# A LoRA linear layer on one core: the last row of each partition of the first chunk stored by fifteen small stores, and lora_B loaded in one transfer

## The chip, the core and the metric

The kernel runs on one core of a Trainium2 chip. The metric is the device time in microseconds (us), the median of several runs: 164.36 us before the change (three runs, 164.32 to 164.52).

The core has five engines with queues of their own: PE (TensorE, matrix products), DVE (VectorE), ACT (ScalarE), POOL (GpSimd) and SP (SyncE, which here only issues transfers). Transfers between DRAM and the core's memory (SBUF) are done by sixteen DMA engines. An engine that issues a transfer goes on at once; the transfer adds to a semaphore when it has landed, 16 in all.

## What is computed

```
x_flat = x.reshape(-1, 256)              # 32768 rows
y = x_flat @ W                           # W: 256 x 256
lora_out = ((x_flat @ lora_A) * lora_E) @ lora_B      # rank 16
y = y + scale * lora_out                 # float32, scale = 1
```

x and the output are 33.55 MB each. The weights are small: W is 256 KB, lora_A and lora_B 16 KB each, lora_E 64 bytes.

## The kernel before

**One weight.** A prologue folds the low-rank path into W: lora_A is transposed on PE (L125), scaled by lora_E on DVE (`ate`, L129), multiplied by lora_B on PE (L134) and added to W (`weff`, L138). Then each row of x takes one product with `weff`.

**Chunks and slots.** The rows are cut into nine chunks (`PLAN`, L5): the first and last have 16 rows for each of the 128 partitions (2 MB), the seven between have 32 (4 MB). In chunk i, partition p holds `b = PLAN[i]` consecutive rows of 256 floats, so what one partition loads or stores is one run of 16 or 32 KB in DRAM and in SBUF (`rows_of`, L46). There are six slots of 32 rows (L56). A chunk is loaded into its slot, and its result overwrites it there (L201) and is stored from it.

**Inside a chunk** the work goes by groups of 4 rows: DVE rounds 8 rows to bf16 (L148), PE transposes 4 (L162), DVE copies the transposed rows from PSUM (L154), PE multiplies (L173), ACT copies the result from PSUM to the slot (L201).

**The order of the transfers** is written out by hand. All big ones are issued by SP, into one queue (q1 in the profile), which spreads each over the sixteen DMA engines, 8 packets of 16 or 32 KB and a 4-byte packet for the semaphore on each; each engine takes its packets in order.

- SP first issues W (L101) and loads 0 to 5 (`load`, L88), all six slots, in the first 4.5 us.
- Then, as chunks are finished, it waits for ACT's last copy of chunk i and issues store i (`store`, L91).
- After store 2 it issues loads 6, 7 and 8 (`AFTER`, L8). Each takes the slot of chunk 0, 1 or 2, so SP waits first until that store has landed (L212).
- Then come stores 3 to 8, and at the end SP waits for all stores (L94, L224).

ACT issues the small loads on a second queue (q10): lora_A (L102), lora_B in four transfers over rows 0 to 1, 2 to 4, 5 to 8 and 9 to 15 (`B_PARTS`, L12 and L103), and lora_E (L105). DVE waits for lora_B before L121 and for lora_E before L129.

`Count` (L18) keeps a semaphore and the total that was added to it so far; `by` adds to it when an instruction or transfer is done.

Of the kernel before, what the change touches and what calls it, by code (L numbers as in the profile page):

```python
# [4 lines left out]
PLAN = [16] + [32] * 7 + [16]  # L5
ROWS, SLOTS = 32, 6
# [2 lines left out]

G, ROUND = 4, 4  # L10

B_PARTS = [(0, 2), (2, 5), (5, 9), (9, 16)]  # L12
P = 128
FP32 = mybir.dt.float32
BF16 = mybir.dt.bfloat16
# [15 lines left out]
def kernel(tc, x, W, lora_A, lora_B, lora_E, scale, out):  # L31
    nc = tc.nc
    x_flat = x.flatten_outer_dims()
    out_flat = out.flatten_outer_dims()
# [11 lines left out]
    def rows_of(flat, i):  # L46
        b, r0 = PLAN[i], starts[i]
        return flat[r0:r0 + b * P, :].rearrange("(p b) k -> p b k", b=b)
# [28 lines left out]
    s_st = [Count(nc, f"s_st{i}") for i in range(len(PLAN))]  # L77
# [6 lines left out]
    def slot(i):  # L84
        return slots[i % SLOTS][:, :PLAN[i], :]

    def load(i):
        s_ld[i].by(nc.sync.dma_start(out=slot(i), in_=rows_of(x_flat, i)), 16)  # L88

    def store(i):  # L90
        s_st[i].by(nc.sync.dma_start(out=rows_of(out_flat, i), in_=slot(i)), 16)  # L91

    def spent(engine, count):
        engine.wait_ge(count.sem, count.total).then_inc(count.sem, -count.total)  # L94
# [5 lines left out]
    with tc.tile_critical(no_gpsimd_drain=True):  # L100
        s_w.by(nc.sync.dma_start(out=w_sb, in_=W.rearrange("(c p) m -> p c m", p=P)), 16)  # L101
        s_a.by(nc.scalar.dma_start(out=a_sb, in_=lora_A.rearrange("(c p) r -> p c r", p=P)), 16)  # L102
        for lo, hi in B_PARTS:  # L103
            s_b.by(nc.scalar.dma_start(out=b_sb[lo:hi, :], in_=lora_B[lo:hi, :]), 16)
# [9 lines left out]
        out=ident, in_=ident, compare_op=mybir.AluOpType.not_equal, fill=1.0, base=0,  # L114
# [9 lines left out]
    for c in range(KC):  # L124
# [5 lines left out]
        out=ate, in0=ps_at, scalar1=e_sb, scalar2=float(scale),  # L130
# [68 lines left out]
    for g, (i, r) in enumerate(groups):  # L199
        nc.scalar.wait_ge(s_m.sem, g + 1)  # L200
        y = nc.scalar.copy(out=slot(i)[:, r:r + G, :], in_=ps_y[g % 2])  # L201
        if r + G < PLAN[i]:
            y.then_inc(can_y, 1)
        else:
            done = s_y.by(y)
            if g + 1 < NG:
                nc.scalar.wait_ge(s_y.sem, done)
                nc.scalar.sem_inc(can_y, 1)
            nc.sync.wait_ge(s_y.sem, done)
            store(i)  # L210
            for later in AFTER.get(i, []):
                nc.sync.wait_ge(s_st[later - SLOTS].sem, 16)  # L212
                load(later)


# [44 lines left out]
```

## Time and profile before

| | us |
|---|---|
| median of three runs | 164.36 (164.32 to 164.52) |
| the profiled execution | 164.26 |
| its span, first to last instruction | 162.86 |
| PE, DVE, ACT busy | 92.9, 79.3, 66.1 |
| store 0 issued; landed on the first and the last DMA engine | 24.82; 62.52 and 64.97 |
| load 6 issued | 64.99 |
| store 8 issued; landed on the first and the last DMA engine | 129.44; 159.37 and 162.82 |

The profile is that of one execution. Its page gives the busy time of each engine, and the span in 40 slices of 4.07 us, where a digit is the busy share in tenths. "DMA" is the mean share of the sixteen DMA engines. A row of the waits reads "who waited <- for what: us in total, times, longest". A row of the timeline has the start, the duration, the engine, the line, the operation, and in brackets the idle time before it and what ended it. A row of the windows has a stretch, its length, the busy time of the five rows PE, PEld (PE's weight loads), DVE, ACT and POOL with their instructions, the clock granted to PE, the DMA engines' share (counted by the packets that start in the stretch, so it can pass 1) and GB/s. The trace keeps a record of each DMA packet too: queue, start, duration and bytes.

### The profile page before, as it was taken

The numbers are of one execution on the slowest core, as the hardware profiler recorded it, in microseconds if no ns is written. First come the engines' busy times: TensorE is split into PE (matmuls) and PEld (weight loads), VectorE is DVE, ScalarE is ACT, GpSimd is POOL, SyncE is SP. The second block draws the span as 40 slices with busy tenths as digits, with TensorE's granted clock in tenths as the row PEclk, the third lists the DMA queues.
The fourth block names the chain that finished last, engine by engine and source line by source line (L and its number), as shares of the span: only waits on it lengthen the run. The fifth ranks groups of instructions, "written<-read, shape, count | busy, mean of one in ns | idle before, by whom it ended". The sixth has DMA issues, their size and how long they took to land. (4 is left out here: it accounts for less than half of the span.)

```text
span 162.9 us, 2602 instructions
## 1 busy us (share of the span) xinstructions
PE 92.9 (57%) x1028; PEld 82.0 (50%) x1028; DVE 79.3 (49%) x99; ACT 66.1 (41%) x65; POOL 1.0 (1%) x7
## 2 busy tenths in 40 slices
PE   0104989999999999998000039999999400000000
PEld 0003778898898889887000028889889300000000
DVE  0017589888888988892000082988895100000000
ACT  0300267777777777777000004677777600000000
POOL 0100000000000000000000000000000000000000
PEclk9999999999999999999955555999999975555555
DMA  5999999999999989999999999999999999999992
GB/s 145 421 439 475 402 427 467 394 475 419 394 485 402 386 382 463 427 419 445 427 419 459 419 435 402 443 459 427 427 443 427 423 445 427 427 443 419 406 439 89
DMA packets 3204, 67.45 MB, mean 414 GB/s; under 512 B 624, under 2 KB 896, under 8 KB 896
## 3 DMA queue, kind: packets, MB, share of 16 engines
q1 hardware_dynamic: 2864, 67.37, 97.0%
q10 hardware_dynamic: 336, 0.03, 0.2%
q8 instruction: 1, 0.02, 0.0%
q14 instruction: 3, 0.02, 0.0%
HBM read 33.85 MB, written 33.55 MB: 414 GB/s over the span
## 5 line engine op out<-in xcount | busy, mean ns | idle before, releaser
L201 ACT COPY xy<-psum_y 128x1024 f32<-128x1024 f32 x64 | 64.8, 1012 | 57.7 <-PE psum_y L173 57.7
L173 PE MATMUL psum_y<-weff,xt 128*128 128x256 bf16 x512 | 68.8, 279 | 21.7 <-PEq L97 20.1
L173 PEld LDWEIGHTS psum_y<-weff,xt 128*128 128x128 bf16 x512 | 47.6, 100 | 29.7 <-issue 24.3
L154 DVE COPY xt<-psum_xt 128x1024 bf16<-128x1024 bf16 x64 | 43.8, 687 | 14.6 <-PE psum_xt L162 14.5
L148 DVE CAST xb<-xy 128x2048 bf16<-128x2048 f32 x32 | 38.9, 1218 | 20.8 <-DMA xy<-in_x_dram 20.8
L162 PE MATMUL psum_xt<-ident_bf,xb 128*128 128x128 bf16 x512 | 40.8, 226 | 2.1 <-PEq L97 2.1
L162 PEld LDWEIGHTS psum_xt<-ident_bf,xb 128*128 128x128 bf16 x512 | 35.7, 102 | 4.2 <-issue 2.5
L121 DVE CAST b_bf<-xb 16x256 bf16<-16x256 f32 x1 | 0.3, 280 | 9.5 <-DMA xb<-in_lora_B_dram 9.5
L125 PE MATMUL ps_at<-ident,a_sb 128*16 128x128 f32 x2 | 0.6, 394 | 6.8 <-POOL ident_bf L117 6.8
L201 ACT ACT_TABLE_LOAD x1 | 1.3, 1283 | 5.6 <-PEq L109 5.6
L125 PEld LDWEIGHTS ps_at<-ident,a_sb 128*16 128x16 f32 x2 | 0.1, 88 | 6.7 <-issue 6.7
L134 PE MATMUL ps_aeb<-b_bf,ate 16*128 16x256 bf16 x2 | 0.6, 400 | 5.0 <-DVE ate L129 5.0
L134 PEld LDWEIGHTS ps_aeb<-b_bf,ate 16*128 16x128 bf16 x2 | 0.1, 106 | 5.5 <-DVE ate L129 5.5
L129 DVE TENSOR_SCALAR ate<-ps_at,e_sb 16x256 bf16<-16x256 f32 x1 | 0.5, 472 | 2.0 <-DMA e_sb<-in_lora_E_dram 2.0
L138 DVE TENSOR_TENSOR weff<-xb,ps_aeb 128x512 bf16<-128x512 f32 x1 | 0.7, 686 | 0.8 <-PE ps_aeb L134 0.8
L113 POOL TENSOR_SCALAR_AFFINE_SELECT ident<-ident 128x128 f32<-128x128 f32 x1 | 0.3, 292 | 0.2 <-POOL ident L111 0.2
L117 POOL CAST ident_bf<-ident 128x128 bf16<-128x128 f32 x1 | 0.3, 289 | 0.1
L111 POOL MEMSET ident<- 128x128 f32 x1 | 0.2, 204 | 5.1 <-POOLq L109 5.1
L241 POOL MEMSET const-bfloat16-1.0<- 128x1 bf16 x1 | 0.1, 101 | 0.0
L241 POOL MEMSET const-uint8-127<- 128x1 uint8 x1 | 0.1, 101 | 0.0
L241 POOL MEMSET const-float32-0.0<- 128x1 f32 x1 | 0.1, 98 | 0.2 <-issue 0.2
L241 POOL MEMSET const-float32-1.0<- 128x1 f32 x1 | 0.1, 99 | 0.0
## 6 DMA issues: line engine op xcount, KB each, us to landing
xy<-in_x_dram SPq DMA_DIRECT2D x7, 4096.0 KB, 29.1
out_dram<-xy SPq DMA_DIRECT2D x7, 4096.0 KB, 36.9
xy<-in_x_dram SPq DMA_DIRECT2D x2, 2048.0 KB, 16.3
out_dram<-xy SPq DMA_DIRECT2D x2, 2048.0 KB, 36.8
xb<-in_W_dram SPq DMA_DIRECT2D x1, 256.0 KB, 2.9
a_sb<-in_lora_A_dram ACTq DMA_DIRECT2D x1, 16.0 KB, 3.1
xb<-in_lora_B_dram ACTq DMA_DIRECT2D x1, 2.0 KB
xb<-in_lora_B_dram ACTq DMA_DIRECT2D x1, 3.0 KB
```

The lines of the kernel that those rows point to most:

```text
L113: s_id.by(nc.gpsimd.affine_select(out=ident, in_=ident, compare_op=mybir.AluOpType.not_equal, fill=1.0, base=0, pattern=[[-1, P]], channel ...
L117: s_id.by(nc.gpsimd.tensor_copy(out=ident_bf, in_=ident))
L125: at_done = nc.tensor.transpose(ps_at[:, c, :], a_sb[:, c, :], ident)
L129: s_v.by(nc.vector.tensor_scalar(out=ate, in0=ps_at, scalar1=e_sb, scalar2=float(scale), op0=mybir.AluOpType.mult, op1=mybir.AluOpType.mult))
L134: aeb_done = nc.tensor.matmul(ps_aeb[:, c, :], ate[:, c, :], b_bf, start=True, stop=True)
L138: s_v.by(nc.vector.tensor_add(out=weff, in0=w_sb, in1=ps_aeb))
L148: nc.vector.tensor_copy(out=xb[t % 2], in_=slot(i)[:, r:r + 2 * G, :]).then_inc(can_t, 1)
L154: nc.vector.tensor_copy(out=xt[g % 2], in_=ps_xt[g % 2]).then_inc(can_m, 1)
L162: done = nc.tensor.transpose(ps_xt[k % 2][:, j, c, :], xb[k // 2 % 2][:, k % 2 * G + j, c * P:(c + 1) * P], ident_bf)
L173: done = nc.tensor.matmul(ps_y[k % 2][:, j, :], xt[k % 2][:, j, c, :], weff[:, c, :], start=(c == 0), stop=(c == KC - 1))
L201: y = nc.scalar.copy(out=slot(i)[:, r:r + G, :], in_=ps_y[g % 2])
L241: nc = _bacc.Bacc("TRN2", target_bir_lowering=False, num_devices=1)
```

## The change

Chunk 0's store becomes sixteen stores: one of the first 15 rows of each of the 128 partitions, and then, for the last row of each partition, fifteen over 15, 14, 13, 12, 11, 10, 9, 9, 8, 7, 6, 5, 4, 3 and 2 partitions, 128 in all. They have one semaphore, so the wait before load 6 is for the total of 256 and no longer for 16. For loads 7 and 8 the total is 16 as before. lora_B is loaded by one transfer over its 16 rows in the place of four. Nothing else differs.

```diff
-B_PARTS = [(0, 2), (2, 5), (5, 9), (9, 16)]
+B_PARTS = [(0, 16)]
+
+SMALL = [15, 14, 13, 12, 11, 10, 9, 9, 8, 7, 6, 5, 4, 3, 2]
...
     def store(i):
-        s_st[i].by(nc.sync.dma_start(out=rows_of(out_flat, i), in_=slot(i)), 16)
+        to, y, b = rows_of(out_flat, i), slot(i), PLAN[i]
+        if i:
+            s_st[i].by(nc.sync.dma_start(out=to, in_=y), 16)
+            return
+        s_st[i].by(nc.sync.dma_start(out=to[:, :b - 1, :], in_=y[:, :b - 1, :]), 16)
+        p = 0
+        for n in SMALL:
+            s_st[i].by(nc.sync.dma_start(out=to[p:p + n, b - 1, :], in_=y[p:p + n, b - 1, :]), 16)
+            p += n
+        assert p == P
...
-                nc.sync.wait_ge(s_st[later - SLOTS].sem, 16)
+                nc.sync.wait_ge(s_st[later - SLOTS].sem, s_st[later - SLOTS].total)
```

## The prediction

> **What bounds the kernel now.** I read the page's slices and queue table first, then the waits of SP, then a table of windows over the tail, and last the single DMA packets.
>
> ```profile
> DMA  5999999999999989999999999999999999999992
> ...
> q1 hardware_dynamic: 2864, 67.37, 97.0%
> ```
>
> The sixteen DMA engines are busy in every slice from the second to the last but one, and SP's queue q1 alone fills 97.0% of their time. PE is at 57% and DVE at 49%. So the kernel is a queue of 67.4 MB; compute matters only if it lets that queue run dry. It doesn't, by SP's own waits:
>
> ```profile
> SPq L91 <- ACT xy L201: 83.5, 7, 19.3
> SPq L88 <- DMA out_dram<-xy: 36.3, 3, 17.6
> ```
>
> SP issues store 0 at 24.82 us, but the packets of the six loads run to 57.3 to 58.6 us. Store 0 therefore lies 32 us behind them on the same rings. The last store is issued at 129.44 us and lands at 162.82. Every SP wait is spent with tens of microseconds of transfers queued.
>
> The end of a full queue is set by its latest engine:
>
> ```profile
> 156.00:159.00 3.00, 0.00 (x0) 0.00 (x0) 0.00 (x0) 0.00 (x0) 0.00 (x0) 0.50 0.99 426
> 159.00:160.00 1.00, 0.00 (x0) 0.00 (x0) 0.00 (x0) 0.00 (x0) 0.00 (x0) 0.50 0.46 197
> 160.00:161.00 1.00, 0.00 (x0) 0.00 (x0) 0.00 (x0) 0.00 (x0) 0.00 (x0) 0.50 0.15 66
> 161.00:162.00 1.00, 0.00 (x0) 0.00 (x0) 0.00 (x0) 0.00 (x0) 0.00 (x0) 0.50 0.11 49
> ```
>
> The last two columns are the engines' busy share and GB/s. From 159 to 160 us most engines finish; after 160 us two or three of sixteen work (0.15, then 0.11, where two are 0.125). The trace's packet records (queue, start, duration, bytes; no engine number) tell who. On one engine a packet starts 3 to 4 ns before its predecessor ends, so the records string into chains, and an engine's place in the order of small transfers shows in its count of 1 KB packets from lora_B: two engines have 4, one 3, one 2, three 1 and nine none, which is what pieces over 2, 3, 4 and 7 rows give if each piece of n rows uses the same first n engines. I call the engines e0 to e15 in that order. Thirteen chains end between 159.0 and 160.0 us. The late ones:
> - **Y**, 162.35 us. It has one 1 KB packet, so it is e4, e5 or e6. Its 32 KB store packets take some 1302 ns instead of 1213 from 59.6 to 77 and from 107.5 to 131 us, when compute runs too: 2.8 us in sum.
> - **X**, 162.19 us. Beside two 8 KB instruction fetches (0.32 and 0.31 us) its next packets took 1867 and 1582 ns, and one at 55.8 us took 2793. By the chains it is e3 or one of e7 to e15; two chains meet in the same nanosecond at 46.3 us, and I can't tell which goes on.
> - A third, 160.85 us, after a 16 KB fetch of 0.96 us.
>
> Span 162.86 us, profiled execution 164.26, median of the runs 164.36: I sum against 164.26 and note that the median lies 0.10 above.
>
> **The change part by part.**
>
> Main part of store 0. Each engine has 8 packets of 15 KB instead of 16. In the packet records 32 KB packets follow each other every 1209.5 ns and 16 KB ones every 607, so a KB is 37.7 ns: 8 x 37.7 = 0.30 us less on every engine.
>
> The fifteen small stores. A store over n partitions gives one 1 KB packet and one 4-byte completion to each of e0 to e(n-1), if it is split as lora_B's pieces were. e0 and e1 get 15 of these pairs, then 14, 13, 12, 11, 10, 9 on e2 to e7, 8 on e8, then 6, 5, 4, 3, 2, 1 and 0 on e15. Price of a pair: 1 KB load packets took 44 to 46 ns mostly (mean 50) and overlap by 3, a completion takes the next packet 6 ns further: 49 ns. No small store to DRAM is in this trace, so it is bounded: below by the rate of big packets, 37.7 + 6 = 44 ns; above by an engine that waits for each completion, which lands 0.37 us after its packet. I take 49, since the rows nearest to it are packets of the same size on the same queue.
> - Y: 12, 11 or 10 pairs: 0.59, 0.54 or 0.49 less 0.30, so +0.29, +0.24 or +0.19 us.
> - X: as e3 13 pairs, +0.34; as e7 9 pairs, +0.14; as e15 none, -0.30.
> - e0: +0.43, from about 159.9 at most: far from the end.
>
> lora_B in one piece: every engine gets one pair. e0, e1 lose three (-0.15), e2 two, e3 one (-0.05), e4 to e6 none, e7 to e15 gain one (+0.05). Y: 0. X: -0.05 or +0.05.
>
> The prologue. Three issues on ACT go (0.26, 0.28, 0.32 us), so lora_E's is issued near 2.1 us, not 3.02, and has fewer packets ahead on e0 to e3. DVE's first steps may come up to some 2 us earlier:
>
> ```profile
> 9.54 0.28 DVE L121 CAST b_bf<-xb 16x256 bf16<-16x256 f32 x1 [9.54 <-DMA xb<-in_lora_B_dram]
> 11.80 0.47 DVE L129 TENSOR_SCALAR ate<-ps_at,e_sb 16x256 bf16<-16x256 f32 x1 [1.98 <-DMA e_sb<-in_lora_E_dram]
> ...
> 19.26 1.23 DVE L148 CAST xb<-xy 128x2048 bf16<-128x2048 f32 x1 [1.65 <-DMA xy<-in_x_dram]
> ```
>
> But DVE waits at 19.26 for load 1, 1.65 us, and from there the order is as before. What is left of it ends in store 0's issue, 32 us ahead of need: 0. Without that cover it would be up to 2 us.
>
> SP's issues. Fifteen more, by lora_B's 0.26 to 0.32 us some 4.5 us, from 25.2 to about 30 us. Behind them waits store 1, which is due at 35.94: 0. If they took over twice as long, store 1 would be issued late, still 25 us ahead of its turn.
>
> The wait for all of store 0 before load 6 (64.99 us): it now counts 256. The last of it was X's at 64.97; e0 ends 0.4 us later from 62.5 to 63.3, so it hardly moves, and stores 1 and 2 (to 84 us) are queued meanwhile: 0.
>
> Sum: Y decides, as e5: 162.35 + 0.24, X at most 162.48. 164.26 + 0.24 = **164.50 us**; on the median's base 164.60. I give 164.5.
>
> [...]
>
> **The rivals.**
> 1. *The small stores are dearer for the engine.* Over 57 ns a pair Y (11 pairs) loses more than 0.33 us. For it: 1 KB packets went up to 241 ns at the start, when all queues were young; and a write to DRAM in this size is not seen. At 100 ns: 11 x 0.10 - 0.30 = +0.80, 165.06. Chance 0.20.
> 2. *Each small store holds its engine until the completion has landed.* This one is on the other side by far: at 0.37 us a pair Y gets 4.07 - 0.30 = +3.8, 168.0; at the 2.1 us from issue to landing, +22.8, 187. It decides from 57 ns on, too. Against it: after the completions of the big stores the next packet starts at once and takes its 1213 ns. [...] Chance 0.07.
> 3. *The late engines' stalls move.* X's 2.8 us and Y's slow packets are events, not work: other packet times may let X miss the bad moment at 55.8 us (1.0 us more than its neighbours) or pay more. Both must shrink to gain, to the third engine's 160.85 at best: 162.8. Likelier some 0.5: 163.8. Chance 0.19 for a gain beyond 0.2%, 0.08 for a loss beyond it (about 165.3), 0.02 for neither.
> 4. *Y is slow only under the profiler and X alone decides.* Then -0.25 to +0.29 us by X's place: 164.1 to 164.65; inside my forecast's own range.
> 5. *The stores aren't split as told.* If those over 13, 11, 7 and 5 rows each went to e0 alone, it would get 36 KB more at 49 ns or less a KB: 1.8 us, to 161.7 at most, still before Y, which would get fewer. It changes little; no chance of its own.
>
> **How the numbers follow.** Forecast with rival 4: 0.44, of which 0.40 within 0.2% (0.33 us, about what a measurement of this kernel can tell from no change) and 0.04 above. Slower: 0.04 + 0.20 + 0.07 + 0.08 = 0.39. Faster: 0.19. Same: 0.40 + 0.02 = 0.42. Range: from 163.7 (half of rival 3's gains below) to 165.5 (rival 2 and a part of 3 above); the forecast's own range is 164.0 to 164.7.
>
> **What would show it.** Packets on q1: 15 KB ones 128, 1 KB ones 128 more, and 128 more completions of 4 bytes. Store 0's small ones land between 62 and 64 us. The windows after 160 us should still show two engines. DVE's L129 before 11.8 us with store 0's issue near 24.8. If small packets take over 57 ns or gaps open between them, rival 1 or 2 holds; if the tail after 160 us is shorter or longer with packets as priced, rival 3. I'd be wrong too if SP fell so far behind that the queue ran dry, seen as a slice under 9.

## The result and the profile after

The changed kernel takes **165.53 us** (median of four runs, 165.47 to 165.58), the kernel before 164.34 in runs beside them. The ratio is 1.0067 (95% interval 1.0052 to 1.0082): slower by 1.2 us, where the forecast was 164.5 and no change that can be measured. The time lies 0.03 us past the upper end of the range (163.7 to 165.5). The profiled execution took 165.47 us, its span 164.1.

The page of the kernel after, in the two lines that carried the reading of before:

```profile
DMA  5999999998999999999999999999999999999991
...
q1 hardware_dynamic: 3120, 67.37, 96.7%
```

The queue still never runs dry: it is the same 67.37 MB, in 256 more packets (128 of 1 KB and 128 completions, as expected). So again the latest engine sets the end, and the windows over the tail show how late it is:

```profile
159.00:160.00 1.00, 0.00 (x0) 0.00 (x0) 0.00 (x0) 0.00 (x0) 0.00 (x0) 0.50 0.65 279
160.00:161.00 1.00, 0.00 (x0) 0.00 (x0) 0.00 (x0) 0.00 (x0) 0.00 (x0) 0.50 0.35 147
161.00:162.00 1.00, 0.00 (x0) 0.00 (x0) 0.00 (x0) 0.00 (x0) 0.00 (x0) 0.50 0.15 66
162.00:163.00 1.00, 0.00 (x0) 0.00 (x0) 0.00 (x0) 0.00 (x0) 0.00 (x0) 0.50 0.15 66
```

From 160 to 161 us the engines' share is 0.35, where it was 0.15: more engines than the three late ones are late now. And the stretch with two engines at work, over by 162.35 us before, lasts to 163.56: the two last chains end at 163.38 and 163.56 us, 1.2 later than X and Y.

Where it was lost shows in the volume moved in the 6 us around and behind the small stores (last column GB/s). Kernel before, then after:

```profile
62.00:68.00 6.00, 5.88 (x71) 5.33 (x69) 5.29 (x8) 4.43 (x5) 0.00 (x0) 1.00 1.06 456
```

```profile
62.00:68.00 6.00, 5.89 (x71) 5.33 (x69) 5.29 (x8) 4.28 (x5) 0.00 (x0) 1.00 1.05 403
```

The share is the same, the engines "busy" all the time, but 53 GB/s less for 6 us are 0.32 MB, at 27 GB/s an engine (32 KB every 1.21 us before) 0.7 us on each of sixteen. The packet records say which packets. The small stores themselves run as priced, a pair of a 1 KB packet and its completion every 48 ns. Then the first two 32 KB packets of store 1 are slow, on nine engines and not on the other seven. Taken in order of size, the losses of the nine in these two packets go from 0.37 to 1.34 us; if these belong to the engines with 8 and with 15 pairs, that is 0.14 us a pair. The latest engine, X, reads its small stores 1 us after all the others, so it is told apart with certainty (it has 13 of them, so it is e3; records as start in us, KB or "completion", ns):

```
64.104   1 KB        46
64.146   completion   9
...                        thirteen such pairs, 48 ns apart
64.683   1 KB        46
64.725   completion   9
64.731  32 KB      1975      (1213 before)
66.703  32 KB      1492
68.191  32 KB      1213
```

The semaphore got X's last increments at 65.82, 66.01, 66.20, 66.39, 66.58, 66.77 and 66.96 us: 0.19 us apart, four times as slow as the pairs were read. The last of them came 2.2 us after its packet was taken up at 64.725.

The prologue did become faster, by more than I had expected, and it came to nothing:

```profile
7.98 0.47 DVE L140 TENSOR_SCALAR ate<-ps_at,e_sb 16x256 bf16<-16x256 f32 x1 [1.86 <-DMA e_sb<-in_lora_E_dram]
...
19.05 1.23 DVE L159 CAST xb<-xy 128x2048 bf16<-128x2048 f32 x1 [5.27 <-DMA xy<-in_x_dram]
```

lora_E is used at 7.98 us, not 11.80, and DVE then waits 5.27 us for load 1 and not 1.65. Store 0 is issued at 25.99 us, 1.2 later than before and not near 24.8; it still lies more than 30 us ahead of its turn.

### The profile page after: what moved, and what is told of

The parts are those of the page before. It is cut to its first block, busy times and chain, and to the rows that moved or that the text cites. A ratio compares the mean times of both kernels' runs of the same rounds, so it can differ in the third digit from the quotient of the medians.

```text
span 164.1 us, 2614 instructions
## 1 busy us (share of the span) xinstructions
PE 93.5 (57%) x1028; PEld 82.3 (50%) x1028; DVE 79.4 (48%) x99; ACT 66.1 (40%) x65; POOL 1.0 (1%) x7
## 3 DMA queue, kind: packets, MB, share of 16 engines
q1 hardware_dynamic: 3120, 67.37, 96.7%
```

## The experiments

**Theory** (what the experiments are to test): a completion behind a small transfer takes its DMA engine about 0.19 us, whatever the records show; a pair is read in 0.048, so with each pair the engine's writing falls 0.142 us behind its reading, some of which is buffered, and what is over stops the next big packets. Fifteen pairs in a row on the low engines are too many. That is my estimate from the kernel after: X's increments 0.19 us apart against pairs every 0.048, and 0.37 us lost by the engine taken to have eight pairs, where 8 x 0.142 is 1.14, which leaves some 0.8 for the buffer. No record shows the buffer itself. **Rivals**: the prologue; the 1 KB writes as such; increments of one semaphore queueing up; later, reading partitions that are other engines' in a full store. Each ratio is to runs of the kernel before taken beside that kernel's own; their medians lie between 164.20 and 164.51 us.

| kernel | us | ratio to before (95%) |
|---|---|---|
| after | 165.53 | 1.0067 (1.0052 to 1.0082) |
| b_only | 164.39 | 1.0002 (0.9988 to 1.0016) |
| small_only | 165.61 | 1.0086 (1.0055 to 1.0118) |
| one_store | 164.44 | 1.0009 (0.9996 to 1.0022) |
| own_sems | 166.85 | 1.0156 (1.0135 to 1.0177) |
| own_sems_first | 166.00 | 1.0109 (1.0087 to 1.0130) |
| by_16 | 165.04 | 1.0049 (1.0032 to 1.0066) |
| by_16_twice | 166.38 | 1.0125 (1.0103 to 1.0147) |
| spread | 164.66 | 1.0028 (1.0013 to 1.0044) |
| small_loads2 | 165.16 | 1.0051 (1.0037 to 1.0065) |
| four_rows | 166.50 | 1.0158 (1.0127 to 1.0188) |
| three_take | 171.67 | 1.0458 (1.0430 to 1.0485) |
| crossing | 166.81 | 1.0120 (1.0085 to 1.0155) |

**Each part alone.** b_only is the kernel before with `B_PARTS = [(0, 16)]`; small_only the kernel after with the four parts.

> The kernel before with lora_B in one transfer and store 0 as it was. Theory (a completion behind a store to DRAM holds the engine's write side 0.19 us, and the fifteen small stores pile up too many of them): no change, 164.3 us within 0.1; DVE's first steps come 3 to 4 us earlier and nothing follows from it. Rival (the loss of 1.2 us comes from the prologue, by other phases of the packets): 165 us or more.

> The kernel after with lora_B in four transfers again. Theory: 165.5 us within 0.1, the first 32 KB packets behind the small stores slow on nine engines as in the kernel after. Rival (the prologue): 164.6 us, that is the 0.24 of the predicted sum alone.

Both are as the theory says, and the rival with the prologue is out: the small stores are the whole loss. In b_only lora_E is used at 7.82 us, and nothing comes of it.

**One store of the last row.**

```diff
-SMALL = [15, 14, 13, 12, 11, 10, 9, 9, 8, 7, 6, 5, 4, 3, 2]
+SMALL = [128]
```

> Store 0 as 15 rows of each partition and then the last row by one store over 128 partitions: on every engine eight 1 KB packets, but one completion. Theory: 8 x 0.043 + 0.006 - 0.30 = +0.05 us, 164.4, no slow packets behind it. Rival (writes of 1 KB to DRAM are slow, not the completions): a stall of some 0.4 us on all engines as on the engine with eight pairs after, 164.8.

Measured 164.44, ratio 1.0009. The window of this kernel:

```profile
62.00:68.00 6.00, 5.87 (x69) 5.24 (x68) 5.17 (x7) 4.49 (x5) 0.00 (x0) 1.00 1.08 458
```

458 GB/s, nothing lost, with the same 128 packets of 1 KB to the same addresses. Small writes as such are out. What is different is that there are 16 completions and not 128, and, if a store over all 128 partitions is always divided alike, that each engine reads partitions that it reads in a full store too.

**A semaphore for each.**

```diff
-        for n in SMALL:
-            s_st[i].by(...)
+        for k, n in enumerate(SMALL):
+            s_sm[k].by(...)
...
+                if later == SLOTS:
+                    for count in s_sm:
+                        nc.sync.wait_ge(count.sem, 16)
                 load(later)
```

> The kernel after, but each small store counts on a semaphore of its own; SP waits for all of them before load 6. Theory (each engine is held by its own completions): 165.5 us, completions of the latest engine still 0.19 us apart. Rival (144 increments of one semaphore queue up, 20 ns each): no stall, the predicted 164.6.

It is 166.85, but by a fault of mine: the fifteen waits that reset these semaphores stood behind the wait for the last store, and ran from 163.98 to 164.98 us. The last store itself landed at 163.97 us, where it landed at 164.03 in the kernel after: the transfers took as long with fifteen semaphores as with one. The kernel own_sems_first has the waits ahead of that one.

> own_sems with the fifteen waits at SP's end moved ahead of the wait for the last store, so that they aren't run after it. Theory (each engine is held by its own completions): 165.5 us as in the kernel after, and the 1.3 us above it of own_sems was those waits. Rival (increments of one semaphore queue up): 164.6.

166.00. The rival is out: the nine engines' slow packets are there as before, and X's increments, on thirteen different semaphores, come 0.18 to 0.19 us apart (65.08, 65.26, 65.44, ... 67.11). Separate semaphores also show single engines: the first arrivals of the fifteen stores step by 0.20 to 0.22 us at first, when all engines are at it, and by 0.17 at the end, when four to two are. So the interval depends little on how many engines do the same. That it is 0.5 us above the kernel after is not explained; its last engine lands store 8 at 165.05 us and the last but one at 164.03, where the kernel after has 164.03 and 163.77.

**Eight and sixteen on every engine.** by_16 has `SMALL = [16] * 8`; by_16_twice treats the last two rows so.

> The last row by eight stores over 16 partitions: eight pairs of a 1 KB packet and a completion on every engine, 128 increments of one semaphore as in the kernel after. Theory, with what the engine with eight pairs lost there (0.37 us): 8 x 0.048 - 0.30 = 0.08, together +0.45, 164.8 us, the same stall on all sixteen engines. Rival (increments of one semaphore queue up): 144 of them as after, some 1.2 us, 165.5. Rival (1 KB writes are slow): the same as one_store.

> The last two rows by eight stores over 16 partitions each: 16 pairs on every engine. Theory: a pair lets the write side fall 0.19 - 0.048 = 0.142 us behind, of which some 0.8 us are buffered: 16 x 0.142 - 0.8 = 1.47, and 16 x 0.048 - 0.60 = 0.17: +1.6, 166.0 us. If the loss were a fixed one for a row of small stores: about as by_16.

165.04 and 166.38. All sixteen engines have slow packets now (by_16: up to 1580 ns, then up to 1592; by_16_twice: 2365 to 2739, then 1455 to 1571). Measured from the kernel before beside them (164.20), both lost some 0.4 to 0.5 us more than I expected, but the difference is what tells the price: 166.38 - 165.04 = 1.34 us for eight more pairs on each engine, where 8 x 0.142 + 0.08 = 1.22 was expected, and none by a fixed loss. The slow packets alone lost 0.4 us an engine in the mean in by_16 and 1.6 in by_16_twice; the 1.2 between them is the theory's 8 x 0.142 = 1.14, and 8 x 0.142 - 0.4 leaves 0.7 us that these packets don't show, near the 0.8 that the theory calls buffered. So the slope and the part that isn't seen were about right, and what both times lie above the forecast is not in these packets and not explained. The same 6 us in by_16_twice:

```profile
62.00:68.00 6.00, 5.77 (x70) 5.09 (x68) 5.07 (x8) 4.49 (x5) 0.00 (x0) 1.00 1.07 320
```

**The same eight, not in a row.** Three ahead of store 0's main part, three behind it, two behind store 1.

```diff
...
         if i:
             s_st[i].by(nc.sync.dma_start(out=to, in_=y), 16)
+            if i == 1:
+                small(6, 8)
             return
+        small(0, 3)
         s_st[i].by(nc.sync.dma_start(out=to[:, :b - 1, :], in_=y[:, :b - 1, :]), 16)
+        small(3, 6)
...
```

> by_16 with its eight small stores in three lots: three ahead of store 0's main part, three behind it, two behind store 1. Theory (a backlog of completions that some 0.4 us of buffer can take, 0.142 us each, and that big packets work off): three are 0.43, so nothing or little is lost, and 8 x 0.048 - 0.30 = 0.08: 164.3 to 164.5 us. Rival (each small store costs a fixed 0.1 us more than its packets, wherever it stands): as by_16, 0.8 us over the kernel before, 165.0.

164.66, ratio 1.0028: 0.4 us less than by_16, somewhat more than I expected, and the window is back:

```profile
62.00:68.00 6.00, 5.78 (x68) 5.26 (x69) 5.27 (x7) 4.49 (x5) 0.00 (x0) 1.00 1.07 455
```

About half of by_16's loss is thus the row, not the number: behind three at a time no 32 KB packet takes over 1379 ns, where one of the kernel before takes 1347, so three leave no delay that these packets show. What is left of the loss, 0.3 us where the sum was 0.08, isn't in these packets either.

**Loads in place of stores.** The kernel before, with load 2 cut like the store:

```diff
-        s_ld[i].by(nc.sync.dma_start(out=slot(i), in_=rows_of(x_flat, i)), 16)
+        ...
+        s_ld[i].by(nc.sync.dma_start(out=y[:, :b - 1, :], in_=of[:, :b - 1, :]), 16)
+        for n in SMALL:
+            s_ld[i].by(nc.sync.dma_start(out=y[p:p + n, b - 1, :], in_=of[p:p + n, b - 1, :]), 16)
+            p += n
```

> The kernel before; in the place of a store it is load 2 whose last row of each partition comes by the fifteen small transfers, so that the completions stand behind writes to SBUF. Theory in its narrow form (it is the acknowledgement of a write to DRAM that costs 0.19 us): no slow packets, +0.2 to +0.3 us for the latest engines, 164.5 us. In the wide form (any completion costs that): load 3's first packets slow on nine engines and 165.5 us.

165.16, ratio 1.0051, and load 3's first packets take up to 2318 ns. They are slow on all sixteen engines (1409 ns and more), not on nine as expected. In the windows of before and of this kernel:

```profile
27.00:33.00 6.00, 5.88 (x69) 5.32 (x70) 5.29 (x7) 4.48 (x5) 0.00 (x0) 1.00 1.00 431
```

```profile
27.00:33.00 6.00, 5.67 (x69) 4.99 (x66) 4.70 (x6) 4.49 (x5) 0.00 (x0) 1.00 1.00 355
```

So the narrow form, a cost of writes to DRAM alone, falls: a row of small loads into SBUF holds the engines too (355 GB/s in these 6 us, not 431). Why the engines with few or no small loads are slow here is not shown; the wide form alone doesn't say it.

**Bigger small stores.** The fifteen take the last four rows (`b - 4:`), 4 KB to a packet.

> The fifteen small stores take the last four rows, 4 KB to a packet: a pair is 0.157 us of reading, and 1.21 us leave the main part. Theory (0.19 us is a floor for the time between two completions, not an addition): the backlog is 13 x 0.033 = 0.4 us, under the 0.8 that is buffered; no slow packets; X with 13 pairs +0.84 us, Y up to +0.68, the end 0.7 later: 165.0 us. If a completion adds 0.14 us to any packet: 1 us of stall more, 166.1.

166.50, outside what either said. X's increments are again 0.19 to 0.20 us apart (65.05, 65.24, 65.43, 65.62, 65.82, 66.01, 66.21, 66.40), though its packets are four times as long and follow each other every 0.161 us. So 0.19 is here a floor between completions and no addition: 0.19 us with 1 KB packets, 0.19 to 0.20 with 4 KB. The packets behind agree: on X and the other engines with many small stores, store 1's first packets take 1213 ns, as the theory said. The time has another source: some 4 KB packets took up to 720 ns, and five packets of store 1 are slow (1789 to 2015 ns), those that can be placed on engines with four small stores or fewer. All engines lose again between 80 and 86 us, where loads follow stores. I can't say what of that belongs to the stores; as a time the run tells nothing.

**Less for the late engines, in big packets.** This was to be the better version: e0 to e2, with 2.4 us to spare, take the 12 last rows of partitions 112 to 127 from the others.

```diff
+SMALL = [3, 3, 3, 3, 2, 2]
...
+        s_st[i].by(nc.sync.dma_start(out=to[:112, :, :], in_=y[:112, :, :]), 16)
+        s_st[i].by(nc.sync.dma_start(out=to[112:, :4, :], in_=y[112:, :4, :]), 16)
+        p = 112
         for n in SMALL:
-            ... to[p:p + n, b - 1, :] ...
+            ... to[p:p + n, 4:, :] ...
```

> Work moved in big packets and few completions. Store 0 is one store over 112 partitions (seven 16 KB packets on each engine), one over the other 16 partitions' first 4 rows (a 4 KB packet each), and their 12 other rows by stores over 3, 3, 3, 3, 2 and 2 partitions, which only e0 to e2 take. Theory (the end is set by X and Y, e3 to e6, and completions 0.46 us apart leave no backlog): X and Y lose 0.607 - 0.162 = 0.44 us, e0 and e1 gain 6 x 0.463 - 0.44 = 2.3 and end near 161.9 at the latest: 0.4 us faster than before, 163.9 us. Rival (X and Y are late in the profiled execution only, or the packets of e0 to e2 end last): no gain or a loss.

171.67 us. A 12 KB packet took 1.31 us in the mean (0.46 to 2.55), where those of four_rows take 0.46; three engines read neighbouring partitions, and 3 x 0.46 = 1.38. So here the partitions that an engine reads matter: the three engines at neighbouring partitions took as long as if they shared one rate, 1.31 us a packet against 0.46. Why is not shown. That put a new rival beside the theory, since the small stores read neighbouring partitions too.

**Neighbouring partitions, few completions.** These three stores replace the main part and the small stores of the kernel after.

```diff
...
+        s_st[i].by(nc.sync.dma_start(out=to[:112, :, :], in_=y[:112, :, :]), 16)
+        for odd in range(2):
+            s_st[i].by(nc.sync.dma_start(out=to[112:, odd::2, :], in_=y[112:, odd::2, :]), 16)
```

> Separates the completions from another feature of the small stores, that engines read partitions which in a full store other engines read. Store 0 is one store over partitions 0 to 111 (seven 16 KB packets on each engine) and two over partitions 112 to 127, of the even and of the odd rows: 16 packets of 1 KB on each engine, all from the last sixteen partitions, but two completions. Theory (completions make the backlog): 16 x 0.043 + 2 x 0.006 - 0.607 = +0.09 us, 164.4, no slow packets behind them. Rival (reading other engines' partitions makes the backlog, as the 12 KB packets of three_take with their 1.3 us in place of 0.46 suggest): as by_16_twice, which has 16 such packets with 16 completions, some 2 us slower, 166.4.

166.81, ratio 1.0120: the theory's 164.4 is missed and the rival's 166.4 is met. Reading sixteen neighbouring partitions with sixteen engines costs as much, with two completions on each. But the records show that it does so in another way:

- The 1 KB packets themselves are slow here, up to 321 ns (mean 83), where those of by_16 and of the kernel after take 46 (at most 58).
- Behind them the big packets go on at 1213 ns. Three of 32 KB took over 1330 ns between 60 and 72 us, one of them by 2 ns; by_16_twice, with as many small packets, has 32.
- The last completions land 0.35 us behind their packets, where X's last landed 2.2 us behind in the kernel after.

So here neighbouring partitions hold the small packets themselves (83 ns in the mean, not 46) and leave no row of completions outstanding (0.35 us behind, not 2.2). In the kernel after it is the other way round, and X read its thirteen when no other engine was at a small packet. That the rival's number is met is therefore no evidence for it as the cause of the loss after: what holds X there isn't what holds the engines here. The theory forecast no slow packets behind and had that right, but it had put the sharing at nothing, and that was wrong. No run has many completions on partitions that the engine reads in a full store too, which would be the direct test; that is left open.

## What the prediction had right, and what wrong

The forecast was 1 us too low, and the time came out at the very edge of the range. That it is so near the range is luck: the upper end stood for rival 1 at 100 ns a pair and a part of rival 3 (the prediction says rival 2, whose 168.0 lies far outside), and neither is what happened.

- **What bounds the kernel, and that its latest engine sets the end**: right. All kernels here end with the latest chain of packets, but own_sems, whose end is SP's.
- **Prologue, SP's issues, the wait before load 6, lora_B in one piece: nothing**: right. b_only is at 1.0002. SP issued the fifteen from 26.4 to 31.8 us, and store 1 at 37.4:

```profile
25.99 0.35 SPq L97 DMA_DIRECT2D out_dram<-xy  x1
26.39 5.45 SPq L100 DMA_DIRECT2D out_dram<-xy  x15
37.37 11.47 SPq L95 DMA_DIRECT2D out_dram<-xy  x2
66.97 18.90 SPq L90 DMA_DIRECT2D xy<-in_x_dram  x3
```

 Load 6 follows at 66.97, 2.0 later than before, under the cover of stores 1 and 2. The prediction said that this wait hardly moves; it did move, and cost nothing.
- **Which engines take how many small stores**: right. X shows 13, and the engines with slow packets are nine, as many as have eight stores or more.
- **The price of a pair, 49 ns, "since the rows nearest to it are packets of the same size on the same queue"**: this step failed. The records do show 48 ns, but for X's last completion, 9 ns at 64.725 us, they show when it was taken up: the semaphore got it 2.2 us later. What the pair costs comes after, in the next two big packets. X lost 0.76 + 0.28 = 1.04 us there, beside the 13 x 0.048 = 0.62 of the pairs: 0.13 us a pair on average, for thirteen in a row. The rows that I took were packets with one completion behind sixteen of them, or completions with a big packet between; three 4-byte packets in the trace of before (8.470, 8.476 and 8.482 us, two of them completions) stood 6 ns apart and spoke for a price of nothing, but three in a row leave no mark in spread either, where no 32 KB packet behind them takes over 1379 ns. With 0.13, Y as e5 is 11 x 0.13 - 0.30 = +1.1 us, and the last chain came 1.2 later.
- **Rivals 1 and 2**: the time is 0.5 us above rival 1's (165.06 at 100 ns a pair), the mechanism between them: engines are held behind a row of small stores, as rival 2 says, but by 0.19 us each, half of the 0.37 us of the landing lag, and the first 0.7 to 0.8 us of what builds up is not seen. I had given them 0.27 together. What I held against rival 2, that the packet after a big store's completion starts at once and takes its 1213 ns, is true and says nothing of many in a row. Its 2.1 us from issue to landing are those of lora_B's first piece before, issued at 1.43 us and landed from 3.57; no run shows an engine held that long by each small store.
- **Rival 3**, stalls that move, isn't needed: X's chain ends 1.2 us later, and its pairs and slow packets, less the 0.30 of the main part, come to 1.4.

## What to carry to other kernels

In this queue, which never ran dry, the price of the small stores was not their bytes but what they did to the packets behind them: look at the two big packets that follow (1975 and 1492 ns on X, 1213 before). Thirteen small stores in a row cost the latest engine 0.13 us each, lots of two and three cost little (164.66 us, ratio 1.0028), and one store over 128 partitions with the same small packets cost nothing that could be measured (1.0009). To move work from one DMA engine to another by a store over few partitions didn't pay where those partitions lie side by side: the three engines then took nearly three times as long (1.31 us for 12 KB against 0.46).

## What the runs showed that was not expected

- Completions of small transfers reach the semaphore 0.17 to 0.22 us apart from one engine where stores are taken up in a row, on one semaphore or on many, and 0.19 to 0.20 with 4 KB packets as with 1 KB. The packet records give each of them 9 ns. Small loads hold the engines too (load 3's first packets took 1409 to 2318 ns), but no engine is alone there and the interval can't be read.
- Three engines that read neighbouring partitions took 1.31 us for 12 KB in the mean, where such a packet took 0.46 in four_rows.
- Behind the first fetch of 8 KB of instructions (queue q14, 0.32 to 0.33 us) and behind one near 131 to 139 us (0.31 us), the engine's next 32 KB packet takes 1.6 to 1.9 us, in every kernel here (1867 and 1582 ns before, 1875 and 1653 after). A fetch between the two costs its engine less (1334 ns for the next 32 KB before). By the prediction's chains the two are X's, and no change of the data's transfers has removed them.
- One engine's stores take 1302 ns for 32 KB, not 1213, just while compute runs, in all profiled executions (before from 64.2 to 77.2 and 107.5 to 125.7 us, after from 66.7 to 78.4 and 108.8 to 125.7). Why, and whether it does so without the profiler, was not tried.
